# Triangular inverses of a scan, built from blocks of 16 instead of 32

## The chip, the cores and the metric

The kernel runs on one core of a Trainium2 chip. The metric is the device time of one execution in microseconds; the median of several runs counts. Times inside an execution come from the hardware profiler.

## The reference

Two layers of a transformer-like trunk over 640 tokens (512 latent ones and 128 of context), width 1024. The first has latent attention and retention, the second differential attention and a bidirectional RWKV-7 scan; each layer ends with a gated convolutional feed-forward part. The edit lies in the scan:

```python
def rwkv7_scan(r, decay, k, v, kk, a, s0):
    def step(state, inp):
        r_t, w_t, k_t, v_t, kk_t, a_t = inp
        sa = jnp.einsum('bhvk,bhk->bhv', state, kk_t)
        state = (state * w_t[:, :, None, :] - sa[..., None] * (kk_t * a_t)[:, :, None, :]
                 + v_t[..., None] * k_t[:, :, None, :])
        return state, jnp.einsum('bhvk,bhk->bhv', state, r_t)
    ...
    state, y = lax.scan(step, s0.astype(jnp.float32), xs)
    return jnp.moveaxis(y, 0, 1), state
```

It runs over 8 heads of 64 features, forwards and backwards, once for the context and once for the latent tokens.

## The kernel before, in words

The scan works on chunks of 64 tokens. Inside a chunk every token's correction `sa` depends on the ones before it, which is a triangular system: a strictly triangular 64x64 matrix L per head and chunk, and what the recurrence needs is the inverse of I + L. Two chunks (a token tile of 128) in each of two directions, with 8 heads, are one group: 2 x 2 x 8 = 32 matrices. Five groups (g = 0 to 4) cover the context tile and the four latent tiles. SBUF holds the 32 matrices as 16 slots `s` times two halves of 64 partitions.

Each group passes through four parts, each a generator that yields often:

- `pre(g)` (`rw_pre`) makes decays, scaled keys and the masked products, from which `L` (line 1864) and the operands `hq` are copied. At its end `rw_leaf_a` sends L through DRAM (`ld`, line 1884) so that `LI` (line 1887) has one block of a matrix per partition.
- `lb(g)` (`rw_leaf_b`) inverts the 32x32 diagonal blocks by substitution on VectorE: 31 steps of a product `tmp` (line 1901) and a subtraction in `X` (line 1902). Each block takes two partitions (`par`), 16 columns each. Then `X` and its turned copy `ZI` go through DRAM (`xd`, line 1909; `zd`, line 1908) and come back as `zb` (line 1913) and `X11` (line 1917).
- `lc(g)` (`rw_leaf_c`) joins two 32x32 inverses to one of 64x64, in two halves `hs`: a product with L (line 1933), a copy `tt` (line 1939), a product with the second inverse (line 1943), and the write of `zb` with a minus sign (line 1948). All products go to the PSUM tile `lf`.
- `steps(g, d)` (`rw_step`) runs the recurrence of the group's two chunks; line 1980 is the product with `zb`. Two `zb` tiles serve the groups in turn, and 8 buffers `hq` hold two groups.

In one pass of the loop over groups `weave` advances `steps(g)`, `pre(g + 2)`, `lb(g + 1)` and `lc(g + 1)` together; the pairs of numbers are the part of the pass over which a generator's steps are spread. A background stream (`side_mix`: the q, k, v products of line 1325, then the differential attention of lines 1442 to 1490) is advanced between them at the rates of `BG`. A scheduler then fixes the order of the instructions on each engine; every engine, and SP's queue, works its list in order. SP issues nearly all the transfers.

```python
        weave(bg, BG[0], (pre(0), 0, 1))
        weave(bg, BG[1], (pre(1), 0, 1), (lb(0), 0.1, 0.7), (lc(0), 0.9, 1.0))
        for g in range(5):
            gens = [(steps(g, 0), 0, 1), (steps(g, 1), 0.03, 1)]
            if g + 2 < 5:
                gens.append((pre(g + 2), 0, 1))
            if g + 1 < 5:
                gens += [(lb(g + 1), 0.1, 0.75), (lc(g + 1), 0.9, 1)]
            weave(bg, BG[2 + g], *gens)
```

`RTAG` gives each kind of tile its width and its number of buffers.

## Time and profile before

| | us |
|---|---|
| runs | 2075.40, 2061.55, 2073.32 |
| median | 2073.32 |
| span of the profiled execution | 2059.5 |
| TensorE busy in it | 1952.7 (95%) |
| VectorE busy | 1253.8 (61%) |
| ScalarE busy | 887.3 (43%) |
| GpSimd busy | 186.5 (9%) |

The span runs from the first to the last instruction of the profiled execution; no time from outside is recorded for that execution alone, and the fastest run is 2 us above its span. In the rows below PE is TensorE's matmul, PEld its weight load, DVE VectorE, ACT ScalarE, POOL GpSimd and SPq SyncE's queue. A name such as `lf<-X11h,L` is output and inputs of an instruction; L1933 is a line of the kernel. A matmul of two f32 tiles shows as two instructions.

### The profile page before, as it was taken

The numbers are of one execution on the slowest core, as the hardware profiler recorded it, in microseconds if no ns is written. First come the engines' busy times: TensorE is split into PE (matmuls) and PEld (weight loads), VectorE is DVE, ScalarE is ACT, GpSimd is POOL, SyncE is SP. The second block draws the span as 40 slices with busy tenths as digits, with TensorE's granted clock in tenths as the row PEclk, the third lists the DMA queues.
The fourth block names the chain that finished last, engine by engine and source line by source line (L and its number), as shares of the span: only waits on it lengthen the run. The fifth ranks groups of instructions, "written<-read, shape, count | busy, mean of one in ns | idle before, by whom it ended". The sixth has DMA issues, their size and how long they took to land.

```text
span 2059.5 us, 36275 instructions
## 1 busy us (share of the span) xinstructions
PE 1952.7 (95%) x14376; PEld 1765.7 (86%) x14376; DVE 1253.8 (61%) x2752; ACT 887.3 (43%) x1680; POOL 186.5 (9%) x365
## 2 busy tenths in 40 slices
PE   6999999999999999999989897898779999999999
PEld 3998565999899899999978676777679999999999
DVE  6554657556456465577436856877667764656555
ACT  4433344334244243456333334667534542524343
POOL 1001000000000000000024332332110000000000
PEclk9999999999999999999989998979989999999999
DMA  8237344234543512143264554454453212122221
GB/s 323 67 109 242 105 134 163 89 104 147 181 153 116 192 62 83 60 151 104 83 207 100 109 161 120 100 116 96 100 200 106 77 58 92 60 85 67 77 63 71
DMA packets 190676, 243.60 MB, mean 118 GB/s; under 512 B 90730, under 2 KB 132970, under 8 KB 190508
## 3 DMA queue, kind: packets, MB, share of 16 engines
q1 hardware_dynamic: 184880, 225.87, 35.7%
q0 software_dynamic: 3904, 13.37, 2.2%
q8 instruction: 113, 1.85, 0.4%
q10 hardware_dynamic: 1724, 2.06, 0.3%
q14 instruction: 55, 0.45, 0.1%
HBM read 202.05 MB, written 39.21 MB: 117 GB/s over the span
## 4 chain that ended last, share of the span: by engine, by line
PE 81%; DVE 7%; DMA 6%; ACT 3%; issue 2%; POOL 1%; SPq 0%; ACTq 0%; DVEq 0%; POOLq 0%
PE mm L470 59%; PE qkv L1325 2%; PE ada L541 2%; PE rv L913 1%; PE pv L1130 1%; PE mm L1097 1%; DMA dk<-pt 1%; PE ptr L1120 1%; PE sc L1442 1%; DVE X L1902 1%; DVE tmp L1901 1%; DMA xd<-X 1%; DMA mq<-tr 1%; DMA raw<-ada 1%; PE mm L1098 1%
## 5 line engine op out<-in xcount | busy, mean ns | idle before, releaser
L414 ACT CAST hi<-raw 128x1024 fp32r<-128x1024 f32 (+4 forms) x212 | 195.9, 925 | 574.1 <-PE mm L470 528.6
L470 PE MATMUL mm<-hhi,hi 128*128 128x322 f32 x1648 | 381.0, 312 | 0.0
L470 PE MATMUL mm<-hlo,hi 128*128 128x322 f32 x1648 | 380.3, 311 | 0.0
L470 PE MATMUL mm<-hhi,lo 128*128 128x322 f32 x1648 | 380.1, 311 | 0.0
L470 PEld LDWEIGHTS mm<-hhi,hi 128*128 128x128 f32 x1648 | 278.3, 189 | 8.7 <-issue 6.7
L470 PEld LDWEIGHTS mm<-hlo,hi 128*128 128x128 f32 x1648 | 279.5, 190 | 0.0
L470 PEld LDWEIGHTS mm<-hhi,lo 128*128 128x128 f32 x1648 | 278.6, 189 | 0.0
L415 DVE TENSOR_TENSOR lo<-raw,hi 128x1024 fp32r<-128x1024 f32 (+4 forms) x212 | 226.1, 1067 | 58.7 <-ACT hi L414 36.0
L672 DVE SCALAR_TENSOR_TENSOR x<-mm,ada,x 128x512 f32<-128x512 f32 (+1 forms) x176 | 88.7, 545 | 176.1 <-PE mm L470 175.9
L470 PE MATMUL mm<-ahi,hi 128*128 128x320 f32 x704 | 161.7, 311 | 0.0
L470 PE MATMUL mm<-ahi,lo 128*128 128x320 f32 x704 | 160.7, 309 | 0.0
L470 PE MATMUL mm<-alo,hi 128*128 128x320 f32 x704 | 160.3, 309 | 0.0
L663 DVE COPY shv<-mm 128x2 f32<-128x2 f32 x103 | 16.3, 159 | 207.9 <-PE mm L470 207.9
L470 PEld LDWEIGHTS mm<-ahi,hi 128*128 128x128 f32 x704 | 117.1, 188 | 12.0 <-ACT hi L414 10.1
L1325 PE MATMUL qkv<-w,x 128*128 128x256 f32 x480 | 118.9, 402 | 0.1
L470 PEld LDWEIGHTS mm<-ahi,lo 128*128 128x128 f32 x704 | 117.8, 188 | 0.0
L470 PEld LDWEIGHTS mm<-alo,hi 128*128 128x128 f32 x704 | 117.6, 188 | 0.0
L666 ACT ACTIVATE u<-u,shv 128x128 f32<-128x128 f32 (+1 forms) x176 | 90.3, 557 | 48.8 <-DVE u L665 47.0
L734 DVE SCALAR_TENSOR_TENSOR ac<-u,vt,ac 128x642 f32<-128x642 f32 x88 | 78.0, 887 | 52.5 <-ACT ac L732 52.3
L1325 PEld LDWEIGHTS qkv<-w,x 128*128 128x128 f32 x480 | 94.0, 201 | 17.0 <-issue 1.7
L732 ACT ACTIVATE ac<-u,vt 128x642 f32<-128x642 f32 x88 | 81.3, 925 | 2.8
L665 DVE TENSOR_TENSOR u<-mm,rb 128x128 f32<-128x128 f32 (+1 forms) x176 | 77.3, 481 | 2.5 <-ACT rb L650 2.5
(419 smaller groups left out, 3351.3 us busy)
## 6 DMA issues: line engine op xcount, KB each, us to landing
raw<-ada SPq DMA_DIRECT2D x96, 512.0 KB, 4.6
...
```

The costliest lines, as they stand in the source:

```text
L414: nc.scalar.copy(hi, t)
L415: nc.vector.tensor_tensor(lo, t, hi.bitcast(F32), op=OP.subtract)
L470: nc.tensor.matmul(ps[:, c0 + b:c0 + e], wt[:, ws], at[:, b:e], start=first and j == 0, stop=last and j == 2)
L541: nc.tensor.matmul(ps[32 * j:32 * j + 32, :], self.cs[:, k, :], pieces[j // 2][:, (j % 2) * 512:(j % 2) * 512 + 512], start=k == 0, stop=k ...
L665: nc.vector.tensor_tensor(u[:, o], ps[:, s], rb[:, s], op=OP.mult)
L666: nc.scalar.activation(u[:, o], u[:, o], AF.Identity, bias=sh[:, c:c + 1])
L672: nc.vector.scalar_tensor_tensor(x[:, s], ps[:, s], self.ada_v(l, part, m, c), x[:, s], op0=OP.mult, op1=OP.add)
L732: nc.scalar.activation(ac, u[:, 1:643], AF.Identity, scale=cv[:, 1, f:f + 1], bias=self.vec(f"cb{l}", f))
L734: nc.vector.scalar_tensor_tensor(ac, u[:, 0:642], cv[:, 0, f:f + 1], ac, op0=OP.mult, op1=OP.add)
L913: nc.tensor.matmul(ps[:, :272], at[:, ts], wt[:, k * 272:k * 272 + 272], start=n == 0, stop=n == 23)
L1097: nc.tensor.matmul(sc[:, 0:512], q, kT[:, 0:4], start=True, stop=True)
L1325: nc.tensor.matmul(ps, h[k][:, t * 128:t * 128 + 128], w[k // 4][:, k % 4 * 256:k % 4 * 256 + 256], start=k == 0, stop=k == 7)
```

## The change

The diagonal blocks that VectorE inverts are 16x16 instead of 32x32. A group has 128 of them, one per partition, and the substitution has 15 steps, with at most 64 elements each, instead of 31. `rw_leaf_c` then joins blocks twice: from 16 to 32 with products over 64 rows (the first with `xd`, in which the first block of each pair stands, copied to `ttp`; the second with `zb`, written back with a minus sign), then a product with the identity that turns the 32x32 inverses into `X11`, and from 32 to 64 as before, but for all 16 slots at once. `zb` is set to zero for each group, and the transfers become 8 + 1 before the substitution and 2 + 4 + 8 behind it, instead of 4 + 2 and 2 + 2 + 4. `lb` and `lc` have other parts of a pass, L and LI no longer share a tag, and the numbers of buffers differ. Docstrings and comments are gone, which alters nothing else. The core of the diff (removed lines of the three leaf functions are left out where the functions above show them):

```diff
-NSTEP = {"dense": 64, "mla_proj": 35, "mla_attn": 61, "retention": 30, "ada_side": 18, "pre": 36, "lb": 32, "lc": 5, "steps": 13}
+NSTEP = {"dense": 64, "mla_proj": 35, "mla_attn": 61, "retention": 30, "ada_side": 18, "pre": 36, "lb": 17, "lc": 5, "steps": 13}
...
-    RTAG = {"fs": (1664, 2), "hq": (1792, 8), "t": (512, 7), "kb": (768, 2), "w": (1024, 3), "f": (512, 3), "sv": (512, 4), "g": (256, 7), "pe": (8, 6), "ys": (256, 2), "yv": (256, 2)}
+    RTAG = {"fs": (1664, 2), "hq": (1792, 8), "t": (512, 7), "kb": (768, 2), "w": (1024, 2), "f": (512, 1), "tmp": (64, 1), "sv": (512, 4), "g": (256, 6), "li": (256, 1), "lx": (256, 2), "pe": (8, 6), "ys": (256, 2), "yv": (256, 2)}
...
-        for t in zbs:
+        xds = [self.rd.tile([128, 16, 32], F32, name=f"xd{i}") for i in range(1)]
+        ttp = self.rd.tile([128, 16, 2, 32], F32, name="ttp")
+        for t in xds + [ttp]:
             nc.gpsimd.memset(t, 0.0)
...
         def lb(g):
-            G[g]["X11"] = yield from self.rw_leaf_b(G[g].pop("LI"), G[g]["zb"])
+            yield from self.rw_leaf_b(G[g].pop("LI"), G[g]["zb"], xds[0])
 
         def lc(g):
-            yield from self.rw_leaf_c(G[g].pop("L"), G[g].pop("X11"), G[g]["zb"])
+            yield from self.rw_leaf_c(G[g].pop("L"), G[g]["zb"], xds[0], ttp)
...
-        weave(bg, BG[1], (pre(1), 0, 1), (lb(0), 0.1, 0.7), (lc(0), 0.9, 1.0))
+        weave(bg, BG[1], (pre(1), 0, 1), (lb(0), 0.1, 0.6), (lc(0), 0.8, 1.0))
...
-                gens += [(lb(g + 1), 0.1, 0.75), (lc(g + 1), 0.9, 1)]
+                gens += [(lb(g + 1), 0.1, 0.6), (lc(g + 1), 0.8, 1)]
...
...
+        ld = self.dp.tile([8, 16, 16, 16], F32, name=self.nm("ld"), tag="ld")
+        for b in range(8):
+            nc.sync.dma_start(ld[b].rearrange("s j i -> j s i"), L[b * 16:b * 16 + 16, :, b % 4 * 16:b % 4 * 16 + 16])
+        LI = self.R("LI", 256, "li").rearrange("p (j i) -> p j i", j=16)
+        nc.sync.dma_start(LI, ld.rearrange("g s j i -> (g s) j i"))
         return LI
 
-    def rw_leaf_b(self, LI, zb):
-        nc = self.nc
-        X = self.R("X", 512, "f").rearrange("p (i c) -> p i c", i=32)
+    def rw_leaf_b(self, LI, zb, xd):
+        nc = self.nc
+        X = self.R("X", 256, "lx").rearrange("p (i c) -> p i c", i=16)
         Xf = X.rearrange("p i c -> p (i c)")
         nc.gpsimd.memset(Xf, 0.0)
-        for par in range(2):
-            nc.gpsimd.memset(Xf[64 * par:64 * par + 64, 16 * par:16 * par + 496:33], 1.0)
-        tmp = self.R("tmp", 256, "g")
-        for j in range(31):
-            n, m = j // 2 + 1, 31 - j
+        nc.gpsimd.memset(Xf[:, 0:256:17], 1.0)
+        nc.gpsimd.memset(zb, 0.0)
+        tmp = self.R("tmp", 64, "tmp")
+        for j in range(15):
+            n, m = j + 1, 15 - j
             t = tmp[:, :m * n].rearrange("p (i c) -> p i c", i=m)
             nc.vector.tensor_tensor(t, LI[:, j, j + 1:, None].to_broadcast([128, m, n]), X[:, j:j + 1, 0:n].to_broadcast([128, m, n]), op=OP.mult)
             nc.vector.tensor_tensor(X[:, j + 1:, 0:n], X[:, j + 1:, 0:n], t, op=OP.subtract)
             yield
-        ZI = self.R("ZI", 512, "f").rearrange("p (c i) -> p c i", c=16)
+        ZI = self.R("ZI", 256, "lx").rearrange("p (c i) -> p c i", c=16)
         nc.scalar.copy(ZI, X.rearrange("p i c -> p c i"))
...
+        dx = self.dp.tile([16, 128, 16], F32, name=self.nm("xd"), tag="xd")
+        dz = self.dp.tile([16, 128, 16], F32, name=self.nm("zd"), tag="zd")
+        nc.sync.dma_start(dz.rearrange("c p i -> p c i"), ZI)
+        nc.sync.dma_start(dx.rearrange("i p c -> p i c"), X)
+        for b in range(0, 8, 2):
+            nc.sync.dma_start(xd[b * 16:b * 16 + 16, :, b % 4 * 8:b % 4 * 8 + 16], dx[:, b * 16:b * 16 + 16])
+        for b in range(8):
+            nc.sync.dma_start(zb[b * 16:b * 16 + 16, :, b % 4 * 16:b % 4 * 16 + 16], dz[:, b * 16:b * 16 + 16])
+    def rw_leaf_c(self, L, zb, xd, ttp):
+        nc = self.nc
+        tp = self.PS("lf")
+        for s in range(16):
+            for r in (0, 64):
+                nc.tensor.matmul(tp[r:r + 64, s * 32:s * 32 + 32], L[r:r + 64, s, :], xd[r:r + 64, s, :],
+                                 start=True, stop=True, skip_group_check=True)
+        nc.scalar.copy(ttp[:, :, :, 0:16], tp.rearrange("p (s a c) -> p s a c", s=16, a=2))
+        yield
+        zp = self.PS("lf")
+        tt = ttp.rearrange("p s a c -> p s (a c)")
+        zv = zb.rearrange("p s (a b c) -> p s a b c", a=2, b=2)
+        zpv = zp.rearrange("p (s a c) -> p s a c", s=16, a=2)
+        for s in range(16):
+            for r in (0, 64):
+                nc.tensor.matmul(zpv[r:r + 64, s], tt[r:r + 64, s, :], zv[r:r + 64, s, :, 1], start=True, stop=True, skip_group_check=True)
+        for r in range(0, 128, 32):
+            i = r // 32 % 2
+            nc.vector.tensor_scalar(zv[r:r + 16, :, i, 1], zpv[r:r + 16, :, i], -1.0, None, op0=OP.mult)
+        yield
+        xp = self.PS("lf")
+        for s in range(16):
+            for r in (0, 64):
+                nc.tensor.matmul(xp[r:r + 32, s * 32:s * 32 + 32], zb[r:r + 32, s, 0:32], self.ident[r:r + 32, r:r + 32],
+                                 start=True, stop=True, skip_group_check=True, tile_position=(r, r))
+        X11 = self.R("X11", 512, "f")
+        for r in (0, 64):
+            nc.scalar.copy(X11[r:r + 32], xp[r:r + 32])
+        yield
+        tp = self.PS("lf")
+        for s in range(16):
+            for r in (0, 64):
+                nc.tensor.matmul(tp[r + 32:r + 64, s * 32:s * 32 + 32], L[r:r + 32, s, 32:64], X11[r:r + 32, s * 32:s * 32 + 32],
+                                 start=True, stop=True, skip_group_check=True, tile_position=(r, r + 32))
+        for r in (32, 96):
+            nc.scalar.copy(X11[r:r + 32], tp[r:r + 32])
+        yield
+        zp = self.PS("lf")
+        for s in range(16):
+            for r in (0, 64):
+                nc.tensor.matmul(zp[r:r + 32, s * 32:s * 32 + 32], X11[r + 32:r + 64, s * 32:s * 32 + 32], zb[r + 32:r + 64, s, 32:64],
+                                 start=True, stop=True, skip_group_check=True, tile_position=(r + 32, r))
+        for r in (0, 64):
+            nc.vector.tensor_scalar(zb[r:r + 32, :, 32:64], zp[r:r + 32].rearrange("p (s c) -> p s c", s=16), -1.0, None, op0=OP.mult)
+        yield
```

The order that the scheduler makes of it differs from the scan's beginning on. Three places:

VectorE, the end of group 3's leaf and the beginning of group 4's, before. Lines 1901 and 1902 with `X2310` are group 4's substitution, line 1948 is the last write of group 3's `zb1`, and lines 1445 to 1456 are the background attention.

```order
L1454 RECIPROCAL so2076_12861<-sm2280_14274 128x1
L1445 TENSOR_REDUCE mx2290_14356<-sc2285_14305 128x1
L1901 TENSOR_TENSOR tmp2311_14501<-LI2299_14424,X2310_14497 128x31
L1446 TENSOR_SCALAR mx2290_14356<-mx2290_14356 128x1
L1948 TENSOR_SCALAR zb1_10337<-lf2294_14383 32x8x32 x2
L1902 TENSOR_TENSOR X2310_14497<-X2310_14497,tmp2311_14501 128x31
L1901 TENSOR_TENSOR tmp2311_14501<-LI2299_14424,X2310_14497 128x30
L1453 RECIPROCAL rr2296_14403<-sm2291_14357 128x1
L1902 TENSOR_TENSOR X2310_14497<-X2310_14497,tmp2311_14501 128x30
L1455 SCALAR_TENSOR_TENSOR rr2296_14403<-rr2296_14403,nlam_11883,sm2280_14274 128x1
```

The same place in the changed kernel. `X2309` is group 4's, line 1934 the write of group 3's `zb1` after the join to 32, line 1959 the one after the join to 64:

```order
L1456 SCALAR_TENSOR_TENSOR p2278_14503<-p2289_14627,rr2292_14675,p2278_14503 128x768
L1901 TENSOR_TENSOR tmp2310_14796<-LI2295_14700,X2309_14792 128x15
L1934 TENSOR_SCALAR zb1_10337<-lf2281_14519 16x16x16 x4
L1902 TENSOR_TENSOR X2309_14792<-X2309_14792,tmp2310_14796 128x15
L1901 TENSOR_TENSOR tmp2310_14796<-LI2295_14700,X2309_14792 128x28
...
L1901 TENSOR_TENSOR tmp2310_14796<-LI2295_14700,X2309_14792 128x15
L1902 TENSOR_TENSOR X2309_14792<-X2309_14792,tmp2310_14796 128x15
L1959 TENSOR_SCALAR zb1_10337<-lf2296_14702 32x16x32 x2
L1445 TENSOR_REDUCE mx2306_14786<-sc2305_14783 128x1
```

The substitution stood one or two instructions at a time among the attention's; now its 30 instructions stand together, between two writes of group 3's `zb1`.

TensorE, the joins of group 4 before. `lf2432` and `lf2435` are the joins of group 4, `pa` with line 1971 the first product of group 4's last steps, the rest (`sc`, `ptr`, `pv`) the background attention.

```order
L1472 MATMUL pv2385_14853<-av2326_14590,wT2381_14837 128x128 x6
L1933 MATMUL lf2432_15135<-X11h2433_15136,L2191_13707 32x32 x16
L1467 MATMUL ptr2400_14936<-ident_93,p2374_14812 128x128 x4
L1442 MATMUL sc2390_14877<-ak2332_14596,aq2329_14593 128x512
L1442 MATMUL sc2390_14877<-ak2332_14596,aq2330_14594 128x512
L1442 MATMUL sc2390_14877<-ac2333_14597,aq2329_14593 128x256
L1442 MATMUL sc2390_14877<-ac2333_14597,aq2330_14594 128x256
L1943 MATMUL lf2432_15135<-zb0_10336,tt2434_15155 32x32 x16
L1933 MATMUL lf2435_15176<-X11h2436_15177,L2191_13707 32x32 x16
L1467 MATMUL ptr2401_14944<-ident_93,p2374_14812 128x128 x2
L1943 MATMUL lf2435_15176<-zb0_10336,tt2437_15196 32x32 x16
L1971 MATMUL pa_10320<-SV2383_14844,hq2262_14153 64x64 x8
```

TensorE in the changed kernel, where the first join of group 4 stands (line 1921, `lf2423`). Lines 1948 and 1956 are the last joins of group 3, and line 1992 the product of group 3's steps with `zb1`:

```order
L1467 MATMUL ptr2299_14741<-ident_93,p2235_14212 128x128 x4
L1956 MATMUL lf2296_14702<-zb1_10337,X112286_14620 32x32 x32
L1467 MATMUL ptr2300_14747<-ident_93,p2235_14212 128x128 x2
L1442 MATMUL sc2305_14783<-ak2072_12961,aq2068_12957 128x128
L1442 MATMUL sc2305_14783<-ak2072_12961,aq2069_12958 128x128
L1921 MATMUL lf2423_15363<-xd0_10338,L2188_13925 64x32
L1992 MATMUL pa_10320<-G2304_14773,zb1_10337 64x64
L1472 MATMUL pv2302_14754<-av2067_12956,wT2298_14740 128x128 x6
L1921 MATMUL lf2423_15363<-xd0_10338,L2188_13925 64x32 x5
L1992 MATMUL pa_10320<-G2304_14773,zb1_10337 64x64 x3
L1442 MATMUL sc2311_14799<-ak2073_12962,aq2070_12959 128x128
```

The joins of group 4 stood behind all of group 3's steps, among attention alone; now they begin ahead of the product with group 3's `zb`.

SP, the transfers around group 2's leaf, before (`xd`, `zd`, `X` from `xd`, `zb`, then the `ld` and `LI` of group 3; `fs` is the next input of `pre`, `dy` and `dvt` belong to the steps):

```order
L1909 DMA xd2167_13504<-X2124_13114 128x32x16
L1908 DMA zd2168_13505<-ZI2166_13502 128x16x32
L1917 DMA X112169_13512<-xd2167_13504 32x2x256 x2
L1676 DMA fs2192_13708<-df_8981 128x1664
L1913 DMA zb0_10336<-zd2168_13505 32x16x32 x4
L1884 DMA ld2186_13672<-L2110_13069 32x16x32 x4
L1887 DMA LI2187_13677<-ld2186_13672 64x1024 x2
L2008 DMA dy_8978<-ys2233_13975 512x1x64
```

SP around group 2's leaf in the changed kernel, from its `ld` on:

```order
L1884 DMA ld2099_13137<-L1840_11853 16x16x16 x8
L1886 DMA LI2100_13146<-ld2099_13137 128x256
L1909 DMA xd2152_13509<-X2122_13261 128x16x16
L1908 DMA zd2153_13510<-ZI2151_13507 128x16x16
L2020 DMA dy_8978<-ys2141_13457 512x1x64
L1967 DMA SV2150_13504<-dvt_8977 64x4x64 x2
L1911 DMA xd0_10338<-xd2152_13509 16x16x16 x4
L1913 DMA zb0_10336<-zd2153_13510 16x16x16 x6
L2020 DMA dy_8978<-ys2146_13487 512x1x64
L1913 DMA zb0_10336<-zd2153_13510 16x16x16 x2
L1967 DMA SV2154_13525<-dvt_8977 64x4x64 x2
```

Behind the store of X stand twelve loads instead of six, `zb` in two pieces with a `dy` between them, and the load of `fs` comes behind them all.

## Rows read from the trace of the kernel before

The columns of Rows 1 and 9 are: stretch in us from the span's start, its length, busy us (and instructions) of PE, PEld, DVE, ACT and POOL, the granted clock of TensorE as a share of 2.4 GHz, the mean busy share of the DMA engines, and GB/s. Groups by line give: busy us, mean ns of one, then the idle time before them and what ended it. Rows of one line (Rows 4) give: count, shortest, median and longest ns, first and last start in us, shapes.

**Rows 1.** Busy time by stretch (columns as printed: us, engines, PEclk, DMA, GB/s)

```profile
0.00:1042.00 1042.00, 1007.96 (x6817) 899.58 (x6817) 604.20 (x1233) 430.04 (x738) 39.53 (x109) 1.00 0.41 135
1042.00:1504.00 462.00, 403.89 (x3937) 328.13 (x3937) 303.68 (x942) 233.36 (x602) 135.56 (x221) 0.88 0.50 124
1504.00:2060.00 556.00, 540.86 (x3624) 537.98 (x3622) 345.88 (x578) 223.90 (x341) 11.45 (x35) 0.98 0.25 83
```

**Rows 2.** TensorE's waits in the scan: us in total, times, longest

```profile
PE sc L1442 <- ACT p L1448: 19.6, 15, 6.2
...
PE lf L1933 <- ACT X11h L1929: 4.3, 3, 2.5
...
PE kt L1873 <- DVE zb L1948: 3.4, 4, 1.6
```

**Rows 3.** Chain of waits in the scan, shares by line

```profile
by line: PE qkv L1325 10.3%; DMA dk<-pt 5.5%; issue 5.1%; PE sc L1442 4.8%; DVE X L1902 4.2%; DVE tmp L1901 4.1%; DMA xd<-X 3.9%; PE ptr L1467 2.6%; PE pv L1472 2.5%; DMA dq<-pt 2.5%; DMA LI<-ld 2.3%; ACT p L1448 2.1%; PE sa L1858 2.1%; PE 
```

**Rows 4.** Lines 1884, 1901, 1948, groups 0, 2, 4: ns, start times

```profile
L1884 SPq DMA_DIRECT2D ld<-L x4: 332/504/559, 1119.8 to 1123.7; - x4
...
L1948 DVE TENSOR_SCALAR zb<-lf x4: 403/417/423, 1213.9 to 1219.5; 32x256 f32<-32x256 f32 x4
...
L1884 SPq DMA_DIRECT2D ld<-L x4: 303/402/482, 1288.3 to 1290.5; - x4
...
L1948 DVE TENSOR_SCALAR zb<-lf x4: 402/418/422, 1365.7 to 1370.4; 32x256 f32<-32x256 f32 x4
...
L1884 SPq DMA_DIRECT2D ld<-L x3: 302/487/489, 1424.8 to 1426.3; - x3
...
L1901 DVE TENSOR_TENSOR tmp<-LI,X x31: 175/257/300, 1434.6 to 1469.9; 128x126 f32<-128x126 f32 x3, 128x30 f32<-128x30 f32 x2, 128x56 f32<-128x56 f32 x2, 128x78 f32<-128x78 f32 x2
...
L1948 DVE TENSOR_SCALAR zb<-lf x4: 412/418/422, 1484.6 to 1488.0; 32x256 f32<-32x256 f32 x4
```

**Rows 5.** VectorE's leaf lines 1901, 1902 in the scan, and one shape

```profile
1042.00:1504.00 462.00, 41.32 (x155) 0.88 0.50 124
...
1042.00:1504.00 462.00, 42.80 (x155) 0.88 0.50 124
...
L1901 DVE TENSOR_TENSOR tmp<-LI,X 128x56 f32<-128x56 f32 x10 | 2.2, 217 | 0.2
```

**Rows 6.** DMA issues (KB, us to landing), and SP's time for zb loads

```profile
xd<-X SPq DMA_DIRECT2D x5, 256.0 KB, 6.5
...
dk<-w SPq DMA_DIRECT2D x8, 128.0 KB, 5.2
...
L1913 SPq DMA_DIRECT2D zb<-zd x20: 331/484/674, 1178.9 to 1478.8; - x20
```

**Rows 7.** Products of leaf and steps: groups by shape, then two timeline rows

```profile
L1980 PE MATMUL pa<-G,zb 64*64 64x64 f32 x320 | 16.4, 236 | 0.3
...
L1933 PE MATMUL lf<-X11h,L 32*32 32x32 f32 x320 | 9.1, 208 | 4.3 <-ACT X11h L1929 4.3
L1943 PE MATMUL lf<-zb,tt 32*32 32x32 f32 x320 | 8.7, 214 | 0.5 <-ACT tt L1939 0.5
...
1485.78 0.69 PE L1943 MATMUL lf<-zb,tt 32*32 32x32 f32 x32 [0.47 <-ACT tt L1939]
...
1500.22 0.68 PE L1980 MATMUL pa<-G,zb 64*64 64x64 f32 x16
```

**Rows 8.** Groups by shape: 512-wide reads of PSUM

```profile
L1863 DVE TENSOR_TENSOR hq<-sa,c 128x512 f32<-128x512 f32 x20 | 13.7, 684 | 7.6 <-PE sa L1858 7.3 <-DMA w<-wb_tm 0.2
...
L1804 ACT ACTIVATE ex<-lp 128x512 f32<-128x512 f32 x10 | 6.0, 597 | 6.7 <-PE lp L1800 6.5
```

**Rows 9.** Busy time in three stretches of the scan

```profile
1314.00:1338.00 24.00, 24.00 (x304) 19.66 (x304) 22.07 (x80) 18.86 (x49) 7.50 (x11) 1.00 0.35 89
1338.00:1348.00 10.00, 6.99 (x92) 5.58 (x91) 7.98 (x22) 6.13 (x15) 3.15 (x4) 1.00 0.72 129
1348.00:1358.00 10.00, 10.00 (x52) 8.42 (x51) 5.84 (x12) 5.24 (x12) 2.68 (x6) 0.50 0.61 142
```

More of the change, by code (lines that the diff above doesn't have):

```diff
@@ L1632, in rwkv @@
             self.rd = rc
-            self.rds = {**{t: ra for t in ("fs", "t", "kb", "pe")}, **{t: rb for t in ("w", "f")}, **{t: rc for t in ("hq", "sv", "g", "ys", "yv")}}
+            self.rds = {**{t: ra for t in ("fs", "t", "kb", "pe")}, **{t: rb for t in ("w", "f", "tmp", "li", "lx")}, **{t: rc for t in ("hq", "sv", "g", "ys", "yv")}}
             F["wup"] = [kp.tile([128, 512], F32, name=f"wup{i}") for i in range(2)]
@@ L1903, in rw_leaf_b @@
             yield
-        ZI = self.R("ZI", 512, "f").rearrange("p (c i) -> p c i", c=16)
+        ZI = self.R("ZI", 256, "lx").rearrange("p (c i) -> p c i", c=16)
         nc.scalar.copy(ZI, X.rearrange("p i c -> p c i"))
-        xd = self.dp.tile([32, 128, 16], F32, name=self.nm("xd"), tag="xd")
-        zd = self.dp.tile([16, 128, 32], F32, name=self.nm("zd"), tag="zd")
-        nc.sync.dma_start(zd.rearrange("c p i -> p c i"), ZI)
-        nc.sync.dma_start(xd.rearrange("i p c -> p i c"), X)
@@ L1910, in rw_leaf_b @@
-        for h in range(2):
-            for b in range(2):
-                r0 = h * 64 + b * 32
-                nc.sync.dma_start(zb[r0:r0 + 32, :, b * 32:b * 32 + 32],
-                                  zd.rearrange("c (a g s) i -> (c a) g s i", a=2, g=4)[:, 2 * h + b])
-        X11 = self.R("X11", 512, "f").rearrange("p (a s c) -> p a s c", a=2, s=16)
-        for h in range(2):
-            nc.sync.dma_start(X11[h * 64:h * 64 + 32].rearrange("i a s c -> i a (s c)"),
-                              xd.rearrange("i (a g s) c -> i a g (s c)", a=2, g=4)[:, :, 2 * h])
@@ L1919, in rw_leaf_b @@
-        return X11
-    def rw_leaf_c(self, L, X11, zb):
-        nc = self.nc
-        for hs in range(2):
-            ps = self.PS("lf")
-            tp, zp = ps[:, 0:256], ps[:, 256:512]
-            X11h = self.R("X11h", 256, "g")
-            for h in range(2):
-                r1 = slice(h * 64, h * 64 + 32)
-                nc.scalar.copy(X11h[r1].rearrange("p (s c a) -> p a s c", s=8, a=2), X11[r1, :, hs * 8:hs * 8 + 8])
-            for s in range(8):
-                for h in range(2):
-                    r1, r2 = slice(h * 64, h * 64 + 32), slice(h * 64 + 32, h * 64 + 64)
-                    nc.tensor.matmul(tp[r2, s * 32:s * 32 + 32], L[r1, hs * 8 + s, 32:64], X11h[r1, s * 32:s * 32 + 32],
-                                     start=True, stop=True, skip_group_check=True, tile_position=(h * 64, h * 64 + 32))
-            yield
-            tt = self.R("tt", 256, "g")
-            for h in range(2):
-                r2 = slice(h * 64 + 32, h * 64 + 64)
-                nc.scalar.copy(tt[r2], tp[r2])
-            for s in range(8):
-                for h in range(2):
-                    r1, r2 = slice(h * 64, h * 64 + 32), slice(h * 64 + 32, h * 64 + 64)
-                    nc.tensor.matmul(zp[r1, s * 32:s * 32 + 32], tt[r2, s * 32:s * 32 + 32], zb[r2, hs * 8 + s, 32:64],
-                                     start=True, stop=True, skip_group_check=True, tile_position=(h * 64 + 32, h * 64))
-            yield
-            for h in range(2):
-                r1 = slice(h * 64, h * 64 + 32)
-                nc.vector.tensor_scalar(zb[r1, hs * 8:hs * 8 + 8, 32:64], zp[r1].rearrange("p (s c) -> p s c", s=8), -1.0, None, op0=OP.mult)
```

8 lines of the change are left out of this document (removed).

## Prediction

> **What bounds the kernel now.** I read the stages first. The program has three stretches, and the edit lies in the middle one, the scan, which takes 462 us of the span [rows 1]. There TensorE is busy for 403.9 us, so it stands idle for 58 us; VectorE is busy for 303.7 us. In the stretches around it TensorE idles less (34 us of 1042, 15 us of 556), and nothing there is touched. So the whole question is whether 462 us become shorter.
>
> Next come TensorE's waits in the scan [rows 2]. The longest, 19.6 us, is for the softmax exponentials of the background attention; the leaf (the triangular inverse) accounts directly for 4.3 us before its own products and 3.4 us where the transposes that follow need its PSUM buffer. Added up, that is 7.7 of the 58 us. The chain of waits tells another story [rows 3]: of the chain in the scan 4.2% and 4.1% are the two VectorE lines of the leaf, 3.9% is the transfer of X and 2.3% the load of LI. Of 462 us these are 38.3, 18.0 and 10.6 us. The reader is to see why both are right: the leaf is long, and many times it ends about when everything else does.
>
> Third, how long a leaf lasts, from the first ld transfer to the last write of zb [rows 4]: 1119.8 to 1219.9 (with 0.4 us for the last write), 1288.3 to 1370.8 and 1424.8 to 1488.4, so 100, 82 and 64 us for groups 0, 2 and 4. In group 4 VectorE's part is 1434.6 to 1470, 35 us for 62 instructions that need 17 us by themselves; the rest is other streams' work between them. The next group of the same buffer set can only start its pre when the steps behind the leaf have freed hq, so groups 0, 2 and 4 form one chain with three leaves in it, 246 us of the 384 us from 1120 to 1504.
>
> **The change part by part.**
>
> *VectorE, the substitution.* Out: 310 instructions, 41.3 + 42.8 = 84.1 us [rows 5]. In: 5 groups x 30 = 150 instructions of 15 to 64 elements; the nearest row, 56 elements, has 217 ns, the narrower ones are little shorter, and I take 0.21 us: 32 us. Busy time falls by 52 us. What this is worth on the path: the 38.3 us on the chain shrink in the same ratio, 32/84, to 14.6, a gain of 24 us. Its bounds are 0 (another chain is right behind) and 52 (all of it was waited for).
>
> *Transfers of X and Z.* Out: two stores of 256 KB that land after 6.5 us; in: two of 128 KB. The nearest row of 128 KB from the same queue with a scattered target, dk<-w, has 5.2 us; half of 6.5 would be 3.25. I take 2 us less for each leaf, 10 us in all, of which 8 on the path, as xd<-X is on the chain in 4 of 5 groups. Bounds 0 and 16.
>
> *Transfers issued.* Out 14, in 23 for each group (8 + 1 + 1 + 1 + 4 + 8), each 0.48 us of SP's queue [rows 6]. Four more ld and two more xd less one LI lie ahead of the first product: 5 x 0.48 = 2.4 us; the four additional zb loads land while the first product runs. That is 12 us in five groups, and I count 10, because the order on SP (in the change above) now holds 12 loads between the store of X and whatever stands behind: fs of the next group, dvt rows, dy. Bounds 0 and 22 (all nine on the path).
>
> *The joins.* Out: two halves that overlap, each copy, 16 products, copy, 16 products, write. In: five stages that each need the one before. By themselves they are about 14 us: 2 x 64 instructions at 32 ns and 3 x 64 at 16 ns (8 us with the last one's 0.2 us in each stage; their prices are worked out below), 3 us of copies (the 128x512 copy has 0.60 us; five of them) and 3 us of writes (four like zb<-lf at 0.42, two like the 512-wide 0.68) [rows 4, 7, 8], with a hop between engines at each. The old joins took some 9 us in group 4 with other work between. I take 8 us more for each leaf, 40 us in all. A quarter, 10 us, I put on the path: on TensorE other streams' products stand between the stages, as the order shows, so a stage's wait is mostly covered. If that cover were gone, it would be all 40; if the leaf has slack, 0.
>
> *TensorE, the additional products.* A product of two f32 tiles is two instructions. Out 128, in 320 for each group. At full clock 32 instructions of a 32x32 tile take 0.69 us, less the last one's 0.2 us some 16 ns each; 16 of a 64x64 tile take 0.68 us, some 32 ns each [rows 7]. New: 192 x 16 + 128 x 32 = 7.2 us against 128 x 16 = 2.0; 5.2 us more. By the mean busy time in the scan, with the time at half clock in it, 17.8/640 = 28 ns and 16.4/320 = 51 ns: 11.9 against 3.6, 8.3 us more. If the 64-row products with 32 columns cost as the small ones do, it is 3.1. For five groups that is 15, 26 or 42 us; I take 28. How much of it is on the path is the main choice here. Stretches such as 1314 to 1338 have TensorE busy for 24.00 of 24 us and 1348 to 1358 for 10.00 of 10, and take it whole; 1338 to 1348, at 6.99 of 10, takes it for nothing [rows 9]. I count half, 14 us. Bounds 0 and 42.
>
> Here the Trainium skill, in "TensorE: Matmul & The Clock Gate", section "Wait — 56ns, not 53.3ns?", speaks against the change more than the row does: it says that two matmuls never start less than about 25 ns apart, however few columns they have. The trace disagrees, with 16 ns between instructions of the 32x32 tiles, which alternate between two halves of the array [rows 7]; by the page's 25 ns the addition would be 960 x 25 = 24 us, an estimate, and not the lowest value of 15.
>
> *POOL, ACT, buffers.* POOL gets a memset of zb per group; it is off the path, as POOL is busy for 135.6 of 462 us and idles [rows 1]. ACT's copies come out even (ZI half, joins wider). Tags w and g lose a buffer each; L needs only two at a time. These I count at nothing. What covers them is POOL's and ACT's idle time; if the memset had to wait for steps(g-2) at the head of POOL's queue, kr and rb behind it would be late by that wait.
>
> Sum: -24 - 8 + 10 + 10 + 14 = +2 us. The profiled execution has a span of 2059.5 us, close to the fastest run (2061.55); the other two are 12 and 14 us longer, so the median lies 14 us above the span. I put the sum on the mean of the three, 2070: **2072 us**.
>
> **The rivals.** *A. The leaf was the bound.* The chain of three leaves speaks for it. VectorE's stretch of 35 us falls to 30/62 of it, 17 us, so each leaf is shorter by 18 + 2 - 2.4 - 8 = 10 us, and the ones of groups 0 and 2, with 100 and 82 us, by up to 20; three of them 30 to 50, from which TensorE's additional work takes some back: about -25 us net, 2046. For it: in the new order the joins of group 4 stand among the steps of group 3 instead of behind a stretch of attention alone. Against it: 58 us of idle time must then fall to about 5 (462 - 25 - 404 - 28), unless TensorE also gets its full clock back: in the scan it is granted 0.88 [rows 1], at its lower level (1.2 GHz) in stretches like 1348 to 1358, which began after a stretch with 6.99 of 10 us busy [rows 9]. It decides if the waits of rows 2 shrink by more than TensorE's 28 us.
>
> *B. Two leaves are now coupled on in-order queues, and TensorE pays.* On VectorE one substitution of group 4 stood ahead of the last write of group 3's zb before; now all 30 do. On TensorE a first join of group 4, which waits for xd, stands ahead of the product with group 3's zb. If LI or xd of group 4 lands late, group 3's steps wait, with everything behind them. The loads take 2.4 us longer to issue than before and store plus load of xd some 8 us together. Price: 3 us in each of four pairs, 12, and TensorE's 28 us whole instead of half, 14 more: +2 + 12 + 14 = 28 us, 2098. It decides when xd lands later than the last write of zb before it. Against: before, TensorE waited only 4.3 us for such a load in the whole scan [rows 2].
>
> *C. Nothing is late but in turn.* VectorE's relief, the longer joins and TensorE's work cancel within 1%; this is the forecast.
>
> **How the numbers follow.** C gets 0.47, A 0.26, B 0.27. 1% is 21 us here, about what a measurement of this kernel can tell from no change. The chances of faster, same and slower are these three. C alone reaches from 2054 to 2092. For 8 in 10 the range has to hold the nearer halves of A and B: 2046 to 2100.
>
> **What would show it.** In the profile after: L1901 and L1902 with 150 instructions and about 32 us; the joins with 1600 instructions and 33 to 59 us of TensorE; TensorE busy for about 430 us in the scan. Right if the scan has 455 to 475 us and the chain's VectorE share for the leaf is halved, with TensorE's in its place. A is right if the clock in the scan rises above 0.92 and TensorE idles for less than 40 us. B is right if "lf<-xd" or "tmp<-LI" lead the waits with over 10 us. The prediction fails most likely in the half that I counted of TensorE's work, or in the leaf's slack.

## The result and the profile after

| kernel | runs | median us | lowest to highest | ratio to before, 95% interval |
|---|---|---|---|---|
| before | 5 | 2073.32 | 2061.55 to 2075.4 | |
| after | 5 | 2093.25 | 2090.5 to 2116.04 | 1.0138 [1.0097, 1.0179] |
| after, run again (r1) | 8 | 2094.48 | 2075.65 to 2107.55 | 1.0078 [1.0040, 1.0116] |

The change costs about 20 us, 1%. One of the eight runs of r1 (2107.55 us) was in a slower state and is left out of its ratio and of its row in the table of the experiments. The profiled execution of the first series was its slowest (span 2114.2 us, mean clock 0.948), so the rows below are from r1 (span 2085.4 us, 0.964).

Busy time by stretch, r1: the whole scan; it answers to the second line of [rows 1].

```profile
1045.00:1528.70 483.70, 433.44 (x4896) 356.21 (x4896) 270.83 (x781) 230.44 (x590) 133.64 (x219) 0.88 0.43 106
```

The scan is 21.7 us longer, at the same mean clock. TensorE is busy for 29.5 us more and idles for 50.3 instead of 58 us. VectorE lost 33 us of work, and the scan is longer all the same.

The same view for single lines of r1: VectorE's L1901 and L1902, then TensorE's five joins, L1921, L1931, L1939, L1948, L1956 (for TensorE the second time is its weight loads').

```profile
1045.00:1528.70 483.70, 16.09 (x75) 0.88 0.43 106
1045.00:1528.70 483.70, 15.75 (x75) 0.88 0.43 106
1045.00:1528.70 483.70, 12.92 (x320) 11.31 (x320) 0.88 0.43 106
1045.00:1528.70 483.70, 12.20 (x320) 10.76 (x320) 0.88 0.43 106
1045.00:1528.70 483.70, 8.42 (x320) 7.04 (x320) 0.88 0.43 106
1045.00:1528.70 483.70, 7.24 (x320) 6.53 (x320) 0.88 0.43 106
1045.00:1528.70 483.70, 7.67 (x320) 6.95 (x320) 0.88 0.43 106
```

The substitution fell from 84.1 [rows 5] to 31.8 us. The joins went from 17.8 [rows 7] to 48.5 us, 30.7 more.

How long a leaf lasts, r1, groups 0, 2 and 4: first ld, last write of zb (L1959), and for group 4 the substitution. It answers to [rows 4].

```profile
L1884 SPq DMA_DIRECT2D ld<-L x8: 332/447/555, 1123.6 to 1128.5; - x8
L1959 DVE TENSOR_SCALAR zb<-lf x2: 679/684/689, 1226.6 to 1227.4; 32x512 f32<-32x512 f32 x2
...
L1884 SPq DMA_DIRECT2D ld<-L x8: 325/444/448, 1284.1 to 1287.5; - x8
L1959 DVE TENSOR_SCALAR zb<-lf x2: 671/680/689, 1381.8 to 1382.6; 32x512 f32<-32x512 f32 x2
...
L1884 SPq DMA_DIRECT2D ld<-L x8: 392/450/1553, 1439.1 to 1443.9; - x8
L1901 DVE TENSOR_TENSOR tmp<-LI,X x15: 174/208/226, 1448.2 to 1456.6; 128x15 f32<-128x15 f32 x2, 128x28 f32<-128x28 f32 x2, 128x39 f32<-128x39 f32 x2, 128x48 f32<-128x48 f32 x2
...
L1959 DVE TENSOR_SCALAR zb<-lf x2: 680/684/689, 1505.3 to 1506.0; 32x512 f32<-32x512 f32 x2
```

With the last write, the leaves take 104, 99 and 68 us: none is shorter than before (100, 82, 64). In group 4 the substitution shrank from 35 to 8.6 us, but from its first join's product to its last write it now takes 41.5 us (9.5 before); for all five groups that stretch went from 67 to 143 us.

Waits in r1's scan, TensorE's and then VectorE's for LI (us in total, times, longest), and the chain by line. They answer to [rows 2, 3].

```profile
PE lf L1939 <- DVE zb L1934: 6.6, 2, 6.5
PE bp L1829 <- POOL th L1826: 5.6, 5, 2.1
...
PE lf L1921 <- DMA xd<-xd: 5.3, 1, 5.3
...
PE sc L1442 <- ACT p L1448: 4.4, 8, 1.0
...
DVE tmp L1901 <- DMA LI<-ld: 15.8, 4, 7.1
...
by line: PE qkv L1325 12.5%; issue 5.0%; PE sc L1442 4.5%; PE sb L1861 3.5%; PE pv L1472 3.2%; PE sa L1860 2.9%; DMA dk<-pt 2.2%; SPq L1884 2.1%; PE yp L2014 2.1%; PE kt L1875 2.0%; DVE mx L1445 1.9%; PE pa L2000 1.9%; PE ptr L1467 1.9%; DM
```

VectorE's two lines and the store of X have left the head of the chain, and TensorE's lines took their place. The chain fills the stretch in both kernels, so that a line has left it does not say that time was won. TensorE waits twice for the new leaf, 6.5 and 5.3 us, and much less for the softmax (4.4, was 19.6).

DMA issues of the leaf (KB, median us to landing); they answer to [rows 6].

```profile
LI<-ld SPq DMA_DIRECT2D x5, 128.0 KB, 2.1
xd<-X SPq DMA_DIRECT2D x5, 128.0 KB, 3.1
...
zb<-zd SPq DMA_DIRECT2D x40, 16.0 KB, 3.3
xd<-xd SPq DMA_DIRECT2D x20, 16.0 KB, 2.8
```

### The profile page after: what moved, and what is told of

Its sections match the earlier page's. It is cut to its first block, busy times and chain, and to the rows that moved or that the text cites. A ratio compares the mean times of both kernels' runs of the same rounds, so it can differ in the third digit from the quotient of the medians.

```text
span 2114.2 us, 38092 instructions
## 1 busy us (share of the span) xinstructions
PE 2019.8 (96%) x15336; PEld 1824.3 (86%) x15336; DVE 1222.8 (58%) x2602; ACT 884.0 (42%) x1665; POOL 187.4 (9%) x365
## 4 chain that ended last, share of the span: by engine, by line
PE 84%; DVE 6%; DMA 4%; ACT 3%; issue 1%; SPq 1%; POOL 0%; ACTq 0%; DVEq 0%; POOLq 0%
PE mm L470 59%; PE qkv L1325 3%; PE ada L541 2%; PE rv L913 2%; PE sc L1442 1%; PE pv L1130 1%; PE mm L1097 1%; PE ptr L1120 1%; PE sb L1861 1%; PE pv L1472 1%; PE sa L1860 1%; PE ada L563 1%; PE mm L1098 1%; PE ptr L1467 1%; PE mm L1234 1%
```

## The experiments

One quantity made them readable. Executions of one kernel differ by their granted clock. The ten runs of r4 go from 2063.58 us at a mean clock of 0.964 to 2092.75 us at 0.950. A mean clock that is lower by 0.014 stands for 2x2075x0.014 = 58 us more at the lower level, half clock; half of that, 29 us, is lost, and 29 us is what the two runs differ by. So each run's time multiplied by its mean clock is about the time that it would take at full clock. In the table, "full clock" is the mean of that product less the mean of the same for the runs of before in the same series (before: 1991 to 1994 us, standard error about 1; the others 0.6 to 2.4). The rest of the difference of the means is "clock", so the two columns add up to the difference in time.

The product has a fault: TensorE's idle time at half clock is counted by half as well. In the profiled executions, one of each kernel, that idle time is 19 us in before, 28 in r1, 23 in r2, 30 in r9, 31 in r15, 35 in r7 and 36 in r18. Counted whole, it would raise "full clock" by some 4 us for r1, 2 for r2, 6 for r9 and r15, and 8 to 9 for r7 and r18.

| run | kernel | median us | ratio to before, 95% | full clock | clock |
|---|---|---|---|---|---|
| r1 | after | 2094.48 | 1.0078 [1.0040, 1.0116] | +22.6 | -2.7 |
| r2 | before, joins' products x3 | 2104.79 | 1.0136 [1.0104, 1.0169] | +22.1 | +10.2 |
| r3 | before, 15 of 31 steps | 2067.06 | 0.9970 [0.9948, 0.9991] | -1.5 | -3.0 |
| r4 | after, no join to 32 | 2081.30 | 1.0047 [1.0012, 1.0082] | -4.2 | +13.6 |
| r5 | after, both old spans | 2107.88 | 1.0175 [1.0131, 1.0219] | +22.7 | +13.9 |
| r6 | before, both new spans | 2088.79 | 1.0084 [1.0060, 1.0108] | +4.1 | +13.4 |
| r7 | after, loads of xd, zb x2 | 2122.12 | 1.0238 [1.0196, 1.0281] | +32.9 | +17.1 |
| r8 | r4 with old spans | 2067.24 | 0.9971 [0.9944, 0.9999] | -2.2 | -3.4 |
| r9 | before, no products in the joins | 2064.68 | 0.9972 [0.9950, 0.9993] | -14.1 | +7.2 |
| r10 | before, substitution's new span | 2071.03 | 1.0005 [0.9982, 1.0028] | -2.0 | +1.7 |
| r11 | after, substitution's old span | 2085.20 | 1.0077 [1.0042, 1.0111] | +17.2 | -1.1 |
| r12 | after, joins from 0.7 | 2098.11 | 1.0141 [1.0102, 1.0181] | +19.2 | +7.7 |
| r13 | before, joins' new span | 2090.66 | 1.0088 [1.0058, 1.0118] | +6.8 | +11.3 |
| r14 | r11, joins from 0.85 | 2110.53 | 1.0200 [1.0151, 1.0248] | +24.3 | +6.8 |
| r15 | before, loads of LI, X11, zb x2 | 2092.54 | 1.0104 [1.0060, 1.0148] | +18.0 | +2.0 |
| r16 | r11, loads of xd, zb on ACT's queue | 2095.36 | 1.0112 [1.0065, 1.0158] | +20.5 | +1.0 |
| r17 | before, loads of zb x3 | 2083.37 | 1.0070 [1.0044, 1.0096] | +7.4 | +8.0 |
| r18 | before, loads of LI, X11 x2 | 2105.45 | 1.0175 [1.0114, 1.0236] | +8.9 | +28.3 |

### TensorE's work: r1, r2, r4, r9

r1 is the changed kernel as it is.

> The changed kernel once more, beside the others on the same chip. Both theories expect the ratio measured before, 1.010 to 1.018. Its use is a trace of an ordinary execution: the profiled one had 223 us at half clock in its records, far above the others' mean clock of 0.964 to 0.966, so I expect some 20 us less than 2114 us in this span, with TensorE's half clock at about 150 us.

r2 issues the old joins' products three times:

```diff
-                for h in range(2):
+                for h in (0, 1) * 3:
```

> The kernel before, with each product of its joins issued three times into the same place (1280 more instructions of 32x32 tiles, about 36 us of TensorE at the 28 ns that one had before, as much as the change adds). Theory 1, TensorE is the scan's bound and the joins' products are paid in full: 18 to 36 us more, a ratio of 1.009 to 1.017. Theory 2, the change lost by late loads and coupled queues, and TensorE's products hide in its 58 us of idle time: under 1.004.

r4 is the changed kernel without the products of L1921, L1931 and L1939 and the copies and writes between them; X11 is copied from zb, and `lc` has 3 steps instead of 5.

> The changed kernel without the join from 16 to 32 (960 instructions of TensorE, the copies and writes between them are left out; X11 is copied from zb without the turn). Loads, substitution and the second join stay. Theory 1: some 40 us of TensorE go, and the time falls from 1.014 to 0.990 to 1.000, at or below before. Theory 2: the late loads and the order of two leaves remain, so it stays at 1.006 or above.

r9 takes the products out of the kernel before (the write of zb then reads `tt`):

```diff
-            for s in range(8):     # both loops of products
...
-                nc.scalar.copy(tt[r2], tp[r2])
...
+                nc.scalar.copy(tt[r2], X11h[r1])
```

> The kernel before without the products of its joins (640 TensorE instructions, busy for 17.8 us in the scan); the copies and the writes of zb stay, and the off-diagonal block of the inverse is filled with a copy of X11 in place of the join's result. Theory 1 (the scan is TensorE's work at full clock, 355 us, plus about 50 us that half clock costs, plus about 55 us of idle time, and work that is added or taken away changes the total by its full amount): TensorE's work at full clock 340 to 346 us, 2050 to 2064. Theory 2 (the joins' products lie in TensorE's idle time where the steps stand behind VectorE and transfers, so idle time takes their place): 2065 to 2080.

Busy time in the scans of r2 and r9.

```profile
1048.50:1549.80 501.30, 450.38 (x5217) 369.07 (x5217) 310.48 (x938) 234.10 (x604) 133.23 (x219) 0.84 0.46 112
...
1049.30:1504.00 454.70, 396.71 (x3276) 320.58 (x3276) 303.04 (x929) 231.06 (x595) 134.72 (x219) 0.85 0.50 123
```

In r2 the joins are busy for 42.0 us, 24.3 more than before, and at full clock the kernel is 22.1 us slower. In r9 17.8 us are gone and it is 14.1 faster, or 8 with all of its idle time counted. So at full clock the scan pays most of what the joins occupy TensorE, 0.9 of it in r2 and 0.5 to 0.8 in r9; idle time takes in little of it (51 us in r2, 58 in r9 as before). In the time itself the two lie further apart, 32 us more in the mean for r2 and 7 less for r9, as both have more time at half clock (PEclk 0.84 and 0.85 in the scan against 0.88); why is not shown. r4 says the same of the change itself: without the join to 32 the 22.6 us at full clock become -4.2, so that join costs 27. In the mean time r4 is only 10 us below r1, as its clock is lower; r5 and r8, the same pair with the old spans, differ by 25 at full clock and by 42 in the mean time.

### The substitution: r3

```diff
-        for j in range(31):
+        for j in range(15):
```

`NSTEP` gives `lb` 17 steps, as in the changed kernel.

> The kernel before with only the first 15 of the 31 steps of the substitution (part of the inverse is left out), nothing else altered. Theory 1: VectorE's part of the leaf is not what the scan waits for; within 10 us of before, 0.995 to 1.001. Rival A of the prediction, the leaf is the bound: VectorE has some 40 us less work and each leaf is shorter by over 10 us, so 20 to 40 us less, 0.981 to 0.990. Theory 2 expects about 0.99.

```profile
1044.90:1508.20 463.30, 413.39 (x3936) 335.45 (x3936) 272.94 (x771) 234.21 (x603) 130.91 (x219) 0.86 0.49 121
```

VectorE has 31 us less to do, as in the changed kernel, and the scan's length is the same (463.3 against 462). At full clock the gain is 1.5 us with an error of 1.7, in the mean time 4.5. This is the run that decides on the prediction's largest term.

### The spans: r5, r6, r8, r10 to r14

The change also moved the spans in which the leaf is issued. r6 puts them alone into the kernel before, r10 the substitution's, r13 the joins' (group 0's spans are changed likewise):

```diff
-gens += [(lb(g + 1), 0.1, 0.75), (lc(g + 1), 0.9, 1)]
+gens += [(lb(g + 1), 0.1, 0.6), (lc(g + 1), 0.8, 1)]    # r6; r10: lc from 0.9; r13: lb to 0.75
```

> The kernel before with the spans of the changed one (0.1 to 0.6 and 0.8 to 1); nothing else differs. Theory 1: TensorE's work is the same, so 2065 to 2080. Theory 2 (the spans move the time by themselves): 2085 or more, with new waits of TensorE for the leaf and more time at half clock; or, if they help, under 2062, in which case the change lost more by its own work than the difference of the two kernels shows.

> The kernel before with one of the two span changes that cost it 17 us together: the substitution over 0.1 to 0.6 of a group's steps (was 0.7 for the first group and 0.75), the joins still over 0.9 to 1. Theory 1 (the denser substitution holds up VectorE's other work, and TensorE idles or falls to half clock for it): 2080 to 2090. Theory 2 (it is the joins' span, 0.8 to 1 in place of 0.9 to 1, that costs): 2065 to 2078.

> The kernel before with the other half of the spans' change alone: the joins over 0.8 to 1 of a group's steps instead of 0.9 to 1, the substitution over 0.1 to 0.7 and 0.75 as before. Theory 1 (the place of the joins is what cost 17 us, by a longer wait of TensorE and the half clock behind it): 2080 to 2095, with TensorE's work at full clock still 355 us and 10 us or more of half clock's cost or idle time added. Theory 2 (only the two spans together cost): 2066 to 2078.

The joins' span alone moves the kernel before by 16 us, and about two thirds of that is clock (11.3 of 18.1 us in the mean). The traces show one place. Stretches of r6, then of r10 in the same part of the steps (columns as in [rows 1]):

```profile
1392.00:1397.00 5.00, 5.00 (x67) 4.33 (x68) 4.78 (x21) 3.51 (x11) 3.26 (x5) 1.00 0.46 121
1397.00:1402.00 5.00, 0.85 (x9) 0.62 (x6) 5.00 (x17) 1.79 (x5) 0.72 (x1) 0.94 0.36 79
...
1407.00:1412.00 5.00, 5.00 (x30) 4.34 (x30) 4.23 (x17) 1.98 (x4) 0.39 (x1) 0.50 0.02 5
...
1427.00:1432.00 5.00, 5.00 (x35) 3.39 (x32) 1.85 (x8) 1.88 (x6) 1.72 (x3) 0.50 0.06 13
...
1387.00:1392.00 5.00, 3.21 (x34) 2.39 (x33) 5.00 (x17) 3.74 (x10) 1.86 (x1) 1.00 0.36 79
1392.00:1397.00 5.00, 5.00 (x66) 4.43 (x67) 4.13 (x13) 3.98 (x12) 2.77 (x5) 1.00 0.11 16
```

And the timeline of TensorE there, two rows of r6 and two of r10 (start, us, line, products, in brackets the idle time ahead):

```profile
1401.41 1.22 PE L1442 MATMUL sc<-ak,aq 128*128 128x512 f32 x2 [4.15 <-ACT p L1448]
...
1406.51 2.07 PE L1858 MATMUL sa<-kr,kb 64*128 64x128 f32 x8
...
1389.43 0.43 PE L1827 MATMUL bp<-th,rkb 128*32 128x128 f32 x8 [1.79 <-POOL th L1824]
1389.79 1.16 PE L1858 MATMUL sa<-kr,kb 64*128 64x128 f32 x8
```

In r6 a wait of 4.15 us for the softmax leaves TensorE busy for 0.85 of 5 us, and it is then granted half clock for 31 us, although from 1407 on it is busy throughout: eight products take 2.07 us that take 1.16 in r10, where the wait was 1.79 us and the clock stayed. 31 us at half clock are about 15 us lost, and the table has 13.4. r13 has 27 us at half clock in the same place, behind a wait of 2.55 us. TensorE's work is the same in all three (1896 us in r6, 1897 in r10, 1899 in r13, 1897 in before, over the whole execution, with busy time at half clock counted half). So here the order costs by the clock, for two thirds of the loss or more, and not by work.

The length of a wait alone does not settle it. Another wait of r6, with the two stretches behind it, and then a wait of the kernel before, with a stretch behind it:

```profile
1154.12 0.43 PE L1827 MATMUL bp<-th,rkb 128*32 128x128 f32 x8 [3.66 <-POOL th L1824]
1155.60:1159.00 3.40, 3.40 (x13) 2.73 (x11) 3.40 (x10) 0.00 (x0) 2.29 (x3) 0.51 0.53 215
1159.00:1165.80 6.80, 4.97 (x30) 3.88 (x28) 6.59 (x17) 2.98 (x7) 4.56 (x7) 1.00 0.06 19
...
1346.49 0.73 PE L1442 MATMUL sc<-ak,aq 128*128 128x512 f32 x2 [1.88 <-ACT p L1448]
1370.00:1375.00 5.00, 5.00 (x29) 3.85 (x25) 4.54 (x19) 1.43 (x4) 2.47 (x5) 0.50 0.74 197
```

The 3.66 us in r6 cost 3.4 us at half clock, and the 1.88 us in the kernel before were followed by 27 us of it, from 1348 on [rows 9]. What makes one pause cost 3 us at half clock and another 31, no run shows.

r5 gives the changed kernel both old spans, r11 the substitution's; r14 is r11 with `lc` from 0.85, r12 has `lc` from 0.7 and is else the changed kernel; r8 is r4's kernel with both old spans.

> The changed kernel with the spans of the kernel before: the substitution spreads over 0.1 to 0.75 of a group's steps (0.7 for the first group) instead of 0.1 to 0.6, the joins over 0.9 to 1 instead of 0.8 to 1; the arithmetic and the number of instructions are as in the changed kernel. Theory 1 (the scan pays TensorE's additional products, about 31 us busy, nearly whole, and the order matters little): 2085 to 2100, TensorE busy in the scan for 430 to 440 us. Theory 2 (the loss is in where the leaf's instructions stand, that is the first substitution ahead of the last write of zb and the joins spread among the steps): the time moves by more than 10 us, down to 2070 to 2080 if these spans separate two leaves, or up beyond 2105 if the five stages of the join, pressed into a tenth of the steps, wait for each other.

> The changed kernel without its join of 16x16 to 32x32 blocks (so the off-diagonal 16x16 blocks of the inverse are left out, and X11 is copied from zb instead of being turned on TensorE), as run before with 2081, now with the spans of the kernel before. TensorE has the same number of instructions in its leaf as the kernel before, VectorE half. Theory 1 (what was left of the loss, 9 us, was the clock, which differs from order to order, and not the leaf): 2066 to 2084, and the time goes with the granted clock in the scan. Theory 2 (the spans of the changed kernel cost those 9 us): 2060 to 2072, as fast as the kernel before or faster, at any clock.

> The changed kernel with the substitution's span of the kernel before (0.1 to 0.7 and 0.75), the joins over 0.8 to 1 as in the changed kernel. Theory 1 (the substitution's span costs the changed kernel as it may cost the one before; the joins need their room): 2078 to 2090, faster than the changed kernel by some 8 us. Theory 2 (with 0.05 of a group's steps between the last substitution and the first join, some 4 us, xd lands too late): 2098 to 2115, and TensorE's wait for xd grows beyond 10 us.

> The changed kernel with the joins over 0.7 to 1 of a group's steps in place of 0.8 to 1. Squeezing them into 0.9 to 1, with the substitution drawn out, has cost 14 us. Theory 1 (the five stages wait for each other, and more of other streams' work between them hides the hops): 2080 to 2092. Theory 2 (what is left of the loss is TensorE's work alone): 2088 to 2100, TensorE's work at full clock 380 to 385 us as in the changed kernel.

> The changed kernel with the substitution over 0.1 to 0.7 and 0.75 and the joins over 0.85 to 1; over 0.8 to 1 it took 2085, over 0.9 to 1 it took 2108. Theory 1 (TensorE's work of 383 us and at least 44 us of idle time leave no order that wins): 2085 to 2105. Theory 2 (there is a place for the joins that gives back the whole loss): under 2078.

Under five pairs of spans (r1, r5, r11, r12, r14) the changed kernel costs 17 to 24 us at full clock; without its join to 32 it costs -2 and -4 under two (r8, r4). The medians scatter by 25 us, from 2085 to 2111, mostly with the clock. r11 is the mildest, but not by its waits for the leaf: TensorE waits 3.7 us for xd in r11 and 1.3 us in r14, which is the slowest. The interval of r11 contains r1's ratio.

### The transfers: r7, r15 to r18

```diff
-        for b in range(0, 8, 2):       # loads of xd
+        for b in (0, 2, 4, 6) * 2:     # r7; the loads of zb likewise
...
-        for par in range(2):           # loads of LI
+        for par in (0, 1) * 2:         # r15 and r18; both likewise for X11, r15 also for zb
...
-            nc.sync.dma_start(zb[b * 16 ...]      # r16, xd too
+            nc.scalar.dma_start(zb[b * 16 ...]
```

r17 issues the loads of zb twice more, behind those of X11.

> The changed kernel with each of the 4 loads of xd and 8 loads of zb of a group issued twice: 60 more transfers in five groups, 29 us of SP's queue at 0.48 us each. Theory 1 (TensorE's products are what costs): within 8 us of the changed kernel, 2085 to 2102, TensorE busy as in it. Theory 2 (the transfers' issue and landing are on the path, and the first join waits for xd): four more issues ahead of xd's last landing and eight more behind, 2 us and 4 us in each leaf, so 10 to 30 us more, 2104 to 2124, and the wait of the first join for xd grows from 5 to over 12 us.

> The kernel before with the loads of LI, X11 and zb issued twice: 8 more transfers in each group, 40 in all, 19 us of SP's queue at 0.48 us each. Theory 1 (the transfers' issue is not what the scan waits for; the spread between orders and the clock is): 2066 to 2080. Theory 2 (each issue of the leaf costs its time on SP's queue): 2085 to 2095, which would put the change's 45 additional transfers at 17 to 22 us.

> The changed kernel with the spans that gave 2085 (substitution over 0.1 to 0.7 and 0.75, joins over 0.8 to 1), and the 4 loads of xd and 8 of zb of a group issued from ACT's queue instead of SP's. Theory 1 (the issues on SP cost nothing; on ACT they stand ahead of copies and exponentials): 2085 to 2105. Theory 2 (60 issues on SP's queue are on the path): 2060 to 2078, faster than with all on SP by 10 us or more.

> The kernel before with its 4 loads of zb in each group issued three times, the repeats behind the loads of X11: 40 more transfers in all, 19 us of SP's queue at 0.48 us each, none of them ahead of what the first substitution or the first join waits for. Theory 1 (SP's queue is on the path, whatever is issued): 2085 to 2095, idle time of TensorE in the scan 70 us or more (57.5 in the kernel before). Theory 2 (what costs is the later landing of LI and X11): 2066 to 2080, idle time 53 to 62 us.

> The kernel before with the 2 loads of LI and the 2 of X11 in each group issued twice: 20 more transfers, 10 us of SP's queue, each ahead of the first substitution or the first join. Theory 1 (SP's queue): about half of the 18 us that 40 transfers cost, 2077 to 2085. Theory 2 (the landing of LI and X11): most of the 18 us, 2085 to 2095.

The scan of r15, and waits in its scan and in r18's:

```profile
1047.00:1530.80 483.80, 403.86 (x3942) 327.18 (x3942) 308.95 (x949) 235.71 (x608) 136.42 (x226) 0.88 0.53 131
...
DVE tmp L1901 <- DMA LI<-ld: 19.1, 4, 7.4
...
PE lf L1933 <- ACT X11h L1929: 11.2, 2, 6.3
```

In r15 the loss is idle time of TensorE, 80 us against 58, at the clock of before; in r18 it idles for 71 us, in r17 for 62. By full clock, 20 transfers ahead of the leaf's waits (r18) cost 8.9 us, 40 behind them (r17) 7.4, both together as 40 (r15) 18.0: transfers cost wherever they stand, 0.2 to 0.45 us each, and r18's 36 us in the median are mainly clock. The changed kernel pays alike (r7, 60 transfers, 10 us more than r1). Yet taking 60 off SP's queue (r16) won nothing over r11. Whether the price is SP's queue or the DMA engines stays open, as r16 loads ACT instead.

## Why the prediction was wrong

**The step that failed is VectorE's -24 us.** It shrank the 38.3 us that the substitution holds in the chain [rows 3] by the ratio of busy times, that is, it took time on the chain for time that the scan waits for. r3 made just that cut in the kernel before and won 1.5 us at full clock, 4.5 in the mean. The chain names what ended last, among several that end nearly together; take that away and it goes through another.

The traces show where the saved time went. Group 0's last subtractions and first join, before and then in r1:

```profile
L1902 DVE TENSOR_TENSOR X<-X,tmp x31: 174/264/785, 1130.9 to 1168.9; 128x126 f32<-128x126 f32 x3, 128x30 f32<-128x30 f32 x2, 128x56 f32<-128x56 f32 x2, 128x78 f32<-128x78 f32 x2
L1933 PE MATMUL lf<-X11h,L x64: 191/191/212, 1199.5 to 1212.0; 32*32 32x32 f32 x64
...
L1902 DVE TENSOR_TENSOR X<-X,tmp x15: 164/207/585, 1132.5 to 1141.6; 128x15 f32<-128x15 f32 x2, 128x28 f32<-128x28 f32 x2, 128x39 f32<-128x39 f32 x2, 128x48 f32<-128x48 f32 x2
L1921 PE MATMUL lf<-xd,L x64: 218/219/241, 1202.5 to 1205.6; 64*64 64x32 f32 x64
```

The substitution ends 27 us earlier, and the first join starts 3 us later: it stands at its place among the steps in TensorE's order, and the finished inverse lies ready. From the last subtraction to the first join groups 0 to 3 take 10 to 39 us in the kernel before, 47 to 61 in r1 and 42 to 64 in r3. Some 8 us of that are the way through DRAM, as in group 4. So the leaf had slack in these groups before the change, and the change only made it larger. In group 4 the join follows after 8 to 9 us, before and in r1, and TensorE waits 5.3 us for xd in r1; there the 26 us that the substitution saved were spent again in 32 us of longer joins. With the old spans (r5) group 4's joins take 42.1 us, so it is not the span that draws them out.

**Transfers -8, issues +10.** The store of X lands after 3.1 instead of 6.5 us, a larger cut than the 2 us that I took, but in the chain before it stands in three groups (17.9 of its 18.0 us) and not in the four that I counted. By r15, r17 and r18, 45 more transfers at 0.2 to 0.45 us each would be 9 to 20 us. All three terms together, with the substitution's relief, come to -2 to -4 us at full clock (r8, r4), where the forecast had -22: these are the 20 us by which the sum was wrong. r3 puts 22 of the 24 us on the substitution, which leaves -1 to -3 for the transfers and the issues together against the +2 of the forecast. What each of these two is worth is not shown, as no run has the shorter store alone.

**Joins' stages +10 and TensorE's products +14.** Together 24; r1 less r4 is 27, r5 less r8 25, at full clock. The sum came out right, but in part by luck. By r2 TensorE's products are paid at 0.9 and not at half (by r9 at 0.5 to 0.8), so 30.7 us of them are 15 to 28 us instead of 14; at most 12 us are left for the stages, though these are longer by 15 us for each leaf instead of 8. The busy time was as forecast (48.5 within 33 to 59; 433 against about 430 in the scan).

**The rivals.** A falls: the idle time fell by 8, not by 53 us, and the clock in the scan stayed at 0.88. B had the right time (2098) and half of the mechanism: TensorE pays nearly whole. Its coupling is visible, 5.3 and 6.6 us of waits on TensorE and 15.8 us for LI on VectorE (6.3 before), but TensorE's idle time as a whole did not grow, and r11 has less of these waits (3.7 and 0.8 us, 3.3 of the steps for zb, 11.6 for LI) and is still 17 us slower at full clock. C's cancellation failed for want of a gain to cancel with.

**What the forecast did not have** is that order moves the clock: r6, r13 and r18 lose 11 to 28 us by it with the arithmetic of before (r18 has 20 more transfers). In r1 it plays no part (-2.7 us).

No version beats the kernel before: r10 equals it, and r3, r8 and r9, the only ones below it, leave work out.
